# A hybrid decoder trunk on one core: the local attention's bias table is loaded ahead of the second projection's weights, and GpSimd makes its eight slopes at once

## The chip, the core and the metric

The kernel runs on one core of a Trainium2 chip. TensorE (PE) multiplies matrices, VectorE (DVE) and ScalarE (ACT) do the elementwise work, GpSimd (POOL) does a little of it, and SyncE (SP) issues nearly all transfers from HBM. Each engine works through its own list of instructions in order, and waits on semaphores for the others. The metric is the device time of one execution in microseconds (us), as the median of several. A profile of one execution gives the start and the duration of every instruction.

## The reference

The kernel computes two layers of a decoder trunk on 256 tokens of width 1024, in float32. What matters here is the beginning:

```
x = layer_norm(x, ln_in_g, ln_in_b)
memn = layer_norm(mem, ln_mem_g, ln_mem_b)
for l in range(DEPTH):
    h = x @ w_in[l]
    cq, ckv, kr, nq, kc, vc, ks, vs, kw, vw, gl = jnp.split(h, split_at, axis=-1)
    ...                         # latent attention, and sparse attention with three branches
        s = jnp.einsum('bqgrd,bkgd->bgrqk', qi, kw).astype(jnp.float32) * scale
        s = s - slopes[:, :, None, None] * dist.astype(jnp.float32)
    ...                         # output projection, cross-attention into memn, gated FFN
```

The eight heads of the sparse attention subtract a distance times a slope (one half, one quarter, ... of the distance) from their scores. The kernel holds that as a table of 8 x 256 numbers in each partition, `alibi`, made out of one table of negative distances, `neg`, which it loads as a constant.

## The kernel before

Every float32 matrix product is done as three products of numbers split into a high and a low part. A weight tile of 512 KB (`raw`, four buffers) is loaded by SP (line 122), ACT rounds it to the high part (`hi`, line 130), DVE subtracts to get the low part (`lo`, line 131), and PE multiplies. A `raw` buffer is free again when its `lo` is done, so that DVE's progress decides when SP may issue a later weight transfer.

The head of the program, in the order in which the code calls it:

1. The two token tiles `xn[0]` and `xn[1]` (128 tokens each) are loaded and normalized (`layer_norm`, lines 211 to 240). The reciprocal root of the variance is one GpSimd instruction per tile, a power of -0.5 (`rsqrt`, line 209). DVE applies it in line 240, in two halves of 512 columns. The norm of the second tile takes its sums from ACT.
2. PE transposes each half tile (`transposed`, line 247), ACT copies the result as the high part (line 250) and DVE makes the low part (line 251). Eight and six products of ones (`warm`, line 203) keep PE at work meanwhile.
3. The weights of the first projection (`w_kc`, two `raw` tiles) are loaded ahead of layer 0's list, and its products are line 487.
4. Layer 0 then runs a list of named steps written out by hand: `kc nq1 nq0 par k cmp v mem tab qk0 cq qk1 ...`. `nq1` is the second projection. `mem` normalizes the memory tokens (tile `mb`, gain `mg`), with two more GpSimd powers, and `tab` is `load_tables()`, which loads `neg`, makes `alibi` on GpSimd and loads five other tables. `qk0` is the first step that reads `alibi` (line 581).

The order of the code is not the order on the engines: a scheduler places the instructions of each engine by the times that it expects, while data dependencies and free buffers hold. So an instruction that the code calls early may stand between two that it called before.

The lines that the change and the prediction touch:

```
    def rsqrt(o, x):
        G.tensor_tensor(o, x, mhalf, op=ALU.pow)
...
            V.scalar_tensor_tensor(y[:, sl], y[:, sl], mu, g_, op0=sub, op1=ALU.mult)
            V.scalar_tensor_tensor(y[:, sl], y[:, sl], mv[:, 3:4], b_, op0=ALU.mult, op1=ALU.add)
...
        A.activation(h_, x_, AF.Copy)
        V.tensor_tensor(l_, x_, h_.bitcast(F32), op=ALU.subtract)
```

Of the kernel before, what the change touches and what calls it, by code (L numbers as in the profile page):

```python
# [10 lines left out]
F32 = mybir.dt.float32  # L11
# [3 lines left out]
ALU = mybir.AluOpType  # L15
# [3 lines left out]
P = 128  # L19
D = 1024  # L20
S = 256
# [8 lines left out]
HN = 8  # L30
# [59 lines left out]
def trunk(ctx: ExitStack, tc: tile.TileContext, a: dict, out: bass.AP):  # L90
    nc = tc.nc
    V, A, G, T = nc.vector, nc.scalar, nc.gpsimd, nc.tensor
# [4 lines left out]
    tmp = ctx.enter_context(tc.tile_pool(name="tmp", bufs=2))  # L97
# [218 lines left out]
    cok = const.tile([P, NT, HN, 16], F32, name="c_cok", tag="c_cok")  # L316
    alibi = const.tile([P, HN, S], BF16, name="alibi", tag="alibi")

    def load_tables():
        neg = tmp.tile([P, S], F32, name="neg", tag="pT", bufs=4)  # L320
        nc.sync.dma_start(neg, a["c_neg"])
        for h in range(HN):
            G.tensor_scalar(alibi[:, h, :], neg, float(8.0 * 2.0 ** (-(h + 1))), None, op0=ALU.mult)
        nc.sync.dma_start(tri, a["c_tri"])
        nc.sync.dma_start(cs, a["c_cs"])
        nc.sync.dma_start(kcs, a["c_kcs"])
        nc.sync.dma_start(ctab, a["c_ctab"])
        nc.sync.dma_start(cok, a["c_cok"])
# [67 lines left out]
    for l in range(DEPTH):  # L396
# [388 lines left out]
        def mem():  # L785
# [9 lines left out]
            "par": lambda: load_params((0,)),  # L795
            "par2": lambda: load_params((1, 2, 3)),
            "tab": load_tables,
            "cmp": lambda: e.update(vct=compress(e["c2"])),
            "mem": mem,
# [262 lines left out]
```

## Time and profile before

| what | value |
| --- | --- |
| median of three runs | 878.4 us (877.24 to 880.74) |
| the profiled execution | 879.98 us, its span 877.9 us |
| PE busy | 860.3 us, 98% of the span |
| DVE, ACT, POOL busy | 665.2, 532.5, 132.4 us |

The span runs from the first instruction to the last. A timeline row gives the start, the duration, the engine and line, what is written from what, how many instructions were merged, and in brackets how long the engine had stood idle before and what released it. A merged row's duration runs from the start of its first instruction to the end of its last. A windows row gives for a stretch each engine's busy time and the clock that TensorE was granted, 1.00 being 2.4 GHz and 0.50 being 1.2 GHz.

### The profile page before, as it was taken

How to read it: one execution, taken by the hardware profiler on the slowest of the kernel's cores; microseconds unless marked ns; L12 is line 12 of the kernel's file. 1: busy time of each engine (PE TensorE's matmuls, PEld its weight loads, DVE VectorE, ACT ScalarE, POOL GpSimd, SP SyncE). 2: the span in 40 equal slices, each digit the busy share in tenths (PEclk: the TensorE clock that was granted, in tenths of full speed). 3: DMA queues.
4: the chain of work that ended last, by engine and by line, in shares of the span. 5: the costliest groups of instructions: out<-in, count | busy, mean ns of one | idle time of the engine just before them, and what ended most of it. 6: DMA issues, size and time to landing. Idle time of an engine off the chain costs nothing.

```text
span 877.9 us, 14948 instructions
## 1 busy us (share of the span) xinstructions
PE 860.3 (98%) x5502; PEld 766.7 (87%) x5502; DVE 665.2 (76%) x1290; ACT 532.5 (61%) x1014; POOL 132.4 (15%) x140
## 2 busy tenths in 40 slices
PE   8989999999999999999999999999999999999996
PEld 5989798899989888888989998879998888888895
DVE  7789887766578877677688788968566877777777
ACT  5658764555546676666555678636573567667661
POOL 1052000000000332222300020000000033223220
PEclk9989999999999999999999999999999999999998
DMA  7944463476347756656538634446633655665641
GB/s 229 284 145 124 132 173 113 140 251 190 96 123 237 217 158 216 190 165 217 183 110 239 190 90 110 144 127 210 194 119 121 218 159 179 212 192 171 215 142 48
DMA packets 128236, 148.66 MB, mean 169 GB/s; under 512 B 6259, under 2 KB 111009, under 8 KB 128163
## 3 DMA queue, kind: packets, MB, share of 16 engines
q1 hardware_dynamic: 128159, 147.70, 54.5%
q8 instruction: 43, 0.70, 0.3%
q14 instruction: 30, 0.25, 0.1%
q10 hardware_dynamic: 4, 0.01, 0.0%
HBM read 146.64 MB, written 1.05 MB: 168 GB/s over the span
## 4 chain that ended last, share of the span: by engine, by line
PE 91%; DVE 4%; ACT 2%; DMA 2%; issue 1%; POOL 0%; SPq 0%; DVEq 0%; ACTq 0%; POOLq 0%
PE up L259 16%; PE up L261 8%; PE acc L996 5%; PE acc L997 5%; PE acc L998 5%; PE acc L170 3%; PE acc L171 3%; PE acc L169 3%; PE fill L178 2%; PE fill L179 2%; PE xq L179 2%; PE xq L178 2%; PE xq L177 2%; PE fill L171 2%; PE fill L169 2%; PE fill L170 2%
## 5 line engine op out<-in xcount | busy, mean ns | idle before, releaser
L131 DVE TENSOR_TENSOR lo<-raw,hi 128x1024 fp32r<-128x1024 f32 (+5 forms) x296 | 322.8, 1108 | 96.2 <-ACT hi L130 94.0
L130 ACT ACTIVATE hi<-raw 128x1024 fp32r<-128x1024 f32 (+5 forms) x296 | 275.8, 951 | 108.9 <-PE acc L171 34.4
L259 PE MATMUL up<-xT,hi 128*128 128x512 f32 x608 | 152.1, 392 | 0.0
L259 PEld LDWEIGHTS up<-xT,hi 128*128 128x128 f32 x608 | 110.3, 189 | 20.3
L261 PEld LDWEIGHTS up<-xT,lo 128*128 128x128 f32 x608 | 82.9, 190 | 5.9
L984 POOL TENSOR_TENSOR cv<-cv 128x256 f32<-128x256 f32 x40 | 54.2, 1356 | 218.7 <-ACT cv L982 170.0
L261 PE MATMUL up<-xT,lo 128*128 128x256 f32 x608 | 84.8, 282 | 0.0
L978 ACT ACTIVATE cv<-u,par 128x256 f32<-128x256 f32 x76 | 45.4, 598 | 49.6 <-DVE u L971 49.6
L996 PE MATMUL acc<-hi,frh 128*128 128x512 f32 x176 | 68.9, 392 | 0.0
L997 PE MATMUL acc<-lo,frh 128*128 128x512 f32 x176 | 68.8, 391 | 0.0
L998 PE MATMUL acc<-hi,frl 128*128 128x512 f32 x176 | 68.2, 389 | 0.0
L209 POOL TENSOR_TENSOR mv<-mv,mhalf 128x1 f32<-128x1 f32 x16 | 14.3, 897 | 309.0 <-DVE mv L233 158.5
L979 DVE SCALAR_TENSOR_TENSOR cv<-u,par,cv 128x255 f32<-128x255 f32 x76 | 37.6, 495 | 26.4 <-ACT cv L978 26.4
L584 ACT ACTIVATE p<-p,nm 128x128 f32<-128x128 f32 x96 | 42.6, 447 | 9.7 <-DVE nm L581 9.4
L986 ACT ACTIVATE frh<-cv 128x256 fp32r<-128x256 f32 x44 | 18.4, 418 | 37.8 <-POOL cv L984 35.4
L987 POOL TENSOR_TENSOR frl<-cv,frh 128x256 fp32r<-128x256 f32 x40 | 38.0, 952 | 20.3 <-ACT frh L986 20.3
L980 DVE SCALAR_TENSOR_TENSOR cv<-u,par,cv 128x254 f32<-128x254 f32 x76 | 37.9, 498 | 2.5
L998 PEld LDWEIGHTS acc<-hi,frl 128*128 128x128 f32 x176 | 33.0, 188 | 7.5 <-DVE frl L987 0.7
L996 PEld LDWEIGHTS acc<-hi,frh 128*128 128x128 f32 x176 | 33.1, 188 | 7.0 <-ACT frh L986 0.9
L997 PEld LDWEIGHTS acc<-lo,frh 128*128 128x128 f32 x176 | 33.1, 188 | 6.0
L177 PE MATMUL fill<-mTh,hi 128*128 128x256 f32 x128 | 37.2, 291 | 0.0
L179 PE MATMUL fill<-mTh,lo 128*128 128x256 f32 x128 | 36.6, 286 | 0.0
(279 smaller groups left out, 2151.7 us busy)
## 6 DMA issues: line engine op xcount, KB each, us to landing
raw<-in_ffn_w_up SPq DMA_DIRECT2D x88, 512.0 KB, 4.4
raw<-in_ffn_w_down SPq DMA_DIRECT2D x44, 512.0 KB, 4.3
raw<-in_xa_wkv SPq DMA_DIRECT2D x32, 512.0 KB, 3.8
raw<-in_xa_wq SPq DMA_DIRECT2D x16, 512.0 KB, 5.4
raw<-in_xa_wo SPq DMA_DIRECT2D x16, 512.0 KB, 4.2
raw<-in_w_in SPq DMA_DIRECT2D x24, 256.0 KB, 3.4
raw<-in_w_out SPq DMA_DIRECT2D x16, 256.0 KB, 4.6
raw<-in_w_out SPq DMA_DIRECT2D x8, 512.0 KB
```

The source lines that it names most:

```text
L130: A.activation(h_, x_, AF.Copy)
L131: V.tensor_tensor(l_, x_, h_.bitcast(F32), op=ALU.subtract)
L169: T.matmul(o, xh_[:, t, k], h, start=k == 0, stop=False)
L177: T.matmul(o, h[:, ms], xh_[:, :, k], start=k == 0, stop=False)
L179: T.matmul(o, lo[:, ms], xh_[:, :, k], start=False, stop=k == len(ws) - 1)
L259: T.matmul(o, h[:, ms], x2[:, k], start=k == 0, stop=False)
L261: T.matmul(o[:, 0:S], lo[:, ms], x2[:, k, 0], start=False, stop=k == len(ws) - 1)
L978: A.activation(c, u, AF.Identity, bias=pcol("cb", l, ft), scale=w_[2])
L984: E.tensor_tensor(conv[0], conv[0], conv[1], op=ALU.mult)
L996: T.matmul(o, fh[:, ts_], h[:, cs_], start=f == 0, stop=False)
L997: T.matmul(o, fh[:, ts_], lo[:, cs_], start=False, stop=False)
L998: T.matmul(o, fl[:, ts_], h[:, cs_], start=False, stop=f == NF - 1)
```

## The change

The load of `neg` and the eight multiplications that make `alibi` leave `load_tables()`. They now stand in the code just behind the first projection's weights and ahead of layer 0's list, so ahead of the weights of `nq1`.

```diff
     alibi = const.tile([P, HN, S], BF16, name="alibi", tag="alibi")
 
+    neg = tmp.tile([P, S], F32, name="neg", tag="pT", bufs=4)
+    nc.sync.dma_start(neg, a["c_neg"])
+    for h in range(HN):
+        G.tensor_scalar(alibi[:, h, :], neg, float(8.0 * 2.0 ** (-(h + 1))), None, op0=ALU.mult)
+
     def load_tables():
-        neg = tmp.tile([P, S], F32, name="neg", tag="pT", bufs=4)
-        nc.sync.dma_start(neg, a["c_neg"])
-        for h in range(HN):
-            G.tensor_scalar(alibi[:, h, :], neg, float(8.0 * 2.0 ** (-(h + 1))), None, op0=ALU.mult)
         nc.sync.dma_start(tri, a["c_tri"])
```

The same instructions are issued, in another order. On GpSimd, at the head of the program, there stood before (`mv_104` and `mv_129` are the statistics of the first and the second token tile, `mv_716` and `mv_691` those of the memory tiles):

```order
L434 MEMSET kr_190 128x64 x2
L209 ISA
L209 TENSOR_TENSOR mv_104<-mv_104,mhalf_84 128x1 [waits DVE_49]
L209 TENSOR_TENSOR mv_129<-mv_129,mhalf_84 128x1 [waits DVE_49]
L323 TENSOR_SCALAR alibi_179<-neg_744 128x256 [waits DMAHW6_49]
L323 TENSOR_SCALAR alibi_179<-neg_744 128x256 x7
L209 TENSOR_TENSOR mv_716<-mv_716,mhalf_84 128x1 [waits DVE_49]
L209 TENSOR_TENSOR mv_691<-mv_691,mhalf_84 128x1 [waits DVE_49]
```

and there stands now:

```order
L435 MEMSET kr_200 128x64 x2
L209 ISA
L209 TENSOR_TENSOR mv_104<-mv_104,mhalf_84 128x1 [waits DVE_49]
L322 TENSOR_SCALAR alibi_179<-neg_180 128x256 [waits DMAHW7_49]
L322 TENSOR_SCALAR alibi_179<-neg_180 128x256 x7
L209 TENSOR_TENSOR mv_129<-mv_129,mhalf_84 128x1 [waits DVE_49]
L209 TENSOR_TENSOR mv_726<-mv_726,mhalf_84 128x1 [waits DVE_49]
L209 TENSOR_TENSOR mv_701<-mv_701,mhalf_84 128x1 [waits DVE_49]
```

The eight multiplications moved past the power of the second token tile, which now stands behind them and behind the transfer that they wait for.

On VectorE, where the second token tile `x1_74` is finished, there stood before (`lnt_115` and `lnt_122` are the transposed halves of the first tile, `lo_170` is the low part of the first projection's second weight tile):

```order
L251 TENSOR_TENSOR xT_103<-lnt_115,xT_103 128x4x128 [waits Activation_49]
L251 TENSOR_TENSOR xT_103<-lnt_122,xT_103 128x4x128 [waits Activation_49]
L240 SCALAR_TENSOR_TENSOR x1_74<-x1_74,mv_129,fill_99 128x512 [waits DVE_49,Pool_49]
L240 SCALAR_TENSOR_TENSOR x1_74<-x1_74,mv_129,fill_100 128x512 [waits DVE_49]
L131 TENSOR_TENSOR lo_170<-raw_167,hi_169 128x1024 [waits DMAHW6_49]
```

and there stands now:

```order
L251 TENSOR_TENSOR xT_103<-lnt_115,xT_103 128x4x128 [waits Activation_49]
L240 SCALAR_TENSOR_TENSOR x1_74<-x1_74,mv_129,fill_99 128x512 [waits DVE_49,Pool_49]
L251 TENSOR_TENSOR xT_103<-lnt_122,xT_103 128x4x128 [waits Activation_49]
L240 SCALAR_TENSOR_TENSOR x1_74<-x1_74,mv_129,fill_100 128x512 [waits DVE_49]
L131 TENSOR_TENSOR lo_170<-raw_167,hi_169 128x1024 [waits DMAHW6_49]
```

One instruction of the first tile, L251 on `lnt_122`, moved between the two halves of line 240, behind the one that waits for GpSimd; `lo_170` stands behind both as before.

On SP, behind the small tables that follow the first weights, there stood before (`raw_342` is the fourth weight tile from the projections behind the first, `mg_686` the memory norm's gain):

```order
L550 DMA w2_593<-in_nsa_w2_v 128x64 [waits DMAHW5_49]
L337 DMA mg_686<-in_ln_mem_g 128x1024 [waits DMAHW6_49]
L122 DMA raw_342<-in_w_in 128x4x128 [waits DMAHW7_49,DVE_49,Activation_49]
L122 DMA raw_342<-in_w_in 128x4x128 [waits DMAHW0_49]
L122 DMA raw_414<-in_w_in 128x4x128 [waits DMAHW1_49,DVE_49,Activation_49]
```

and there stands now:

```order
L551 DMA w2_603<-in_nsa_w2_v 128x64 [waits DMAHW4_49]
L122 DMA raw_352<-in_w_in 128x4x128 [waits DMAHW7_49,DVE_49,Activation_49]
L122 DMA raw_352<-in_w_in 128x4x128 [waits DMAHW0_49]
L338 DMA mg_696<-in_ln_mem_g 128x1024 [waits DMAHW1_49]
L122 DMA raw_424<-in_w_in 128x4x128 [waits DMAHW2_49,DVE_49,Activation_49]
```

The transfer of `mg` moved behind a weight tile that waits for DVE. The transfer of `neg` stands directly behind the two tiles of `w_kc`, in seventh place of SP's list, where it stood behind the second memory tile before. PE's list is the same as before.

## Rows read from the trace of the kernel before

**Rows 1.** The page: busy time, share of the span, instructions.

```profile
PE 860.3 (98%) x5502; PEld 766.7 (87%) x5502; DVE 665.2 (76%) x1290; ACT 532.5 (61%) x1014; POOL 132.4 (15%) x140
```

**Rows 2.** PE's waits over the span: for whom, us, times, longest.

```profile
PE cmp L523 <- DVE hs L160: 4.0, 2, 3.2
```

**Rows 3.** PE's timeline, 45 to 51 us.

```profile
47.29 0.29 PE L170 MATMUL proj<-lo,xT 128*128 128x280 f32 x1
50.77 0.42 PE L523 MATMUL cmp<-c_ident,hs 34*128 34x34 f32 x2 [3.18 <-DVE hs L160]
```

**Rows 4.** VectorE's timeline, 41 to 52 us.

```profile
44.61 0.69 DVE L220 BATCH_NORM_STATS2 s<-mb 128x6 f32<-128x512 f32 x1 [2.95 <-DMA mb<-in_mem]
...
50.03 0.68 DVE L160 COPY hs<-cmp 34x512 f32<-34x512 f32 x1
50.64 1.81 DVE L131 TENSOR_TENSOR lo<-raw,hi 128x768 fp32r<-128x768 f32 x2
```

**Rows 5.** Stretches: each engine's busy us, TensorE's clock, DMA share, GB/s.

```profile
15.00:20.00 5.00, 4.58 (x32) 3.60 (x31) 5.00 (x8) 2.53 (x5) 0.00 (x0) 1.00 0.55 166
20.00:25.00 5.00, 5.00 (x45) 5.00 (x43) 4.50 (x9) 1.85 (x5) 0.00 (x0) 1.00 0.91 251
...
45.00:50.00 5.00, 2.58 (x21) 2.35 (x19) 4.90 (x7) 2.65 (x4) 4.91 (x5) 0.96 0.89 268
50.00:55.00 5.00, 4.23 (x19) 4.17 (x20) 4.97 (x14) 3.41 (x6) 4.88 (x4) 0.50 0.80 238
55.00:60.00 5.00, 5.00 (x35) 5.00 (x35) 2.78 (x9) 3.21 (x10) 1.34 (x3) 0.85 0.14 48
```

**Rows 6.** SP's timeline, 0 to 60 us: transfers issued.

```profile
16.12 0.43 SPq L337 DMA_DIRECT2D mg<-in_ln_mem_g  x1
17.89 4.52 SPq L122 DMA_DIRECT2D raw<-in_w_in  x6
...
38.07 0.65 SPq L339 DMA_DIRECT2D mb<-in_mem  x1
```

**Rows 7.** GpSimd's timeline, 0 to 60 us, and one multiplication apart.

```profile
12.15 0.56 POOL L209 TENSOR_TENSOR mv<-mv,mhalf 128x1 f32<-128x1 f32 x1 [5.47 <-DVE mv L229]
45.03 10.03 POOL L323 TENSOR_SCALAR alibi<-neg 128x256 bf16<-128x256 f32 x8 [32.32 <-DMA neg<-in_c_neg]
50.68 2.48 POOL L323 TENSOR_SCALAR alibi<-neg 128x256 bf16<-128x256 f32 x1
55.14 1.28 POOL L209 TENSOR_TENSOR mv<-mv,mhalf 128x1 f32<-128x1 f32 x2
```

**Rows 8.** VectorE's timeline, 9 to 20 us.

```profile
9.47 1.23 DVE L131 TENSOR_TENSOR lo<-raw,hi 128x1024 fp32r<-128x1024 f32 x1 [1.39 <-ACT hi L130]
...
14.69 0.69 DVE L251 TENSOR_TENSOR xT<-lnt,xT 128x512 fp32r<-128x512 f32 x1 [0.61 <-ACT xT L250]
15.30 1.40 DVE L240 SCALAR_TENSOR_TENSOR x<-x,mv,fill 128x512 f32<-128x512 f32 x2
16.62 1.22 DVE L131 TENSOR_TENSOR lo<-raw,hi 128x1024 fp32r<-128x1024 f32 x1
```

**Rows 9.** PE's timeline, 10 to 18 us.

```profile
13.03 2.76 PE L203 MATMUL lnt<-ones 128*128 128x512 f32 x6
16.14 1.33 PE L247 MATMUL lnt<-c_ident,x 128*128 128x128 f32 x8 [0.35 <-issue]
17.46 0.74 PE L487 MATMUL projt<-xT,hi 128*128 128x256 f32 x4
```

**Rows 10.** ScalarE's timeline, 0 to 60 us: first weight tiles.

```profile
10.47 1.04 ACT L130 ACTIVATE hi<-raw 128x1024 fp32r<-128x1024 f32 x1
11.72 1.15 ACT L130 ACTIVATE hi<-raw 128x512 fp32r<-128x512 f32 x2 [0.21 <-DMA raw<-in_w_in]
...
25.59 1.06 ACT L130 ACTIVATE hi<-raw 128x1024 fp32r<-128x1024 f32 x1 [1.12 <-DMA raw<-in_w_in]
```

**Rows 11.** The tile alibi: ns shortest, median, longest, first and last start.

```profile
L323 POOL TENSOR_SCALAR alibi<-neg x8: 846/1000/2482, 45.0 to 54.2; 128x256 bf16<-128x256 f32 x8
```

## The prediction

> **What bounds the kernel now.** I read the page first: PE is busy for 860.3 of 877.9 us [rows 1]. So a delay of PE's work is paid in full unless PE would have waited later anyway, and a gain can only come out of PE's waits. The view of waits, second, shows that the largest of them is 4.0 us for the tile hs, 3.2 us of it in one piece [rows 2]. PE's timeline puts that piece at 47.58 to 50.77 us [rows 3]. VectorE's timeline tells why: it stood idle for 2.95 us until the second memory tile had landed at 44.61, and hs stands in its list behind the statistics of that tile and some weight splits, so that it ran only at 50.03 [rows 4]. The windows add the other half of the price: the clock is 0.96 in the stretch 45 to 50, 0.50 in 50 to 55 and 0.85 in 55 to 60 [rows 5]. From 50.77, half the clock for about 5.7 us costs PE some 2.85 us of work. This place, wait and slow stretch, is worth about 6 us, and it hangs on a transfer: the memory tile is issued at 38.07 [rows 6] and lands 6.5 us later.
>
> The multiplications of the bias table end just then, at 55.06, and two powers of the memory norm follow at 55.14 [rows 7]. But PE's 3.2 us wait is for hs and not for them, and nothing on PE waits for the table. What the change takes away from there is worth nothing to PE, or a tenth or two where VectorE's splits run a little faster beside an idle GpSimd.
>
> **The head: GpSimd.** Before, the second token tile's power ran at 12.15 to 12.71 [rows 7], well ahead of its reader: VectorE came to line 240 of that tile at 15.30 without having waited [rows 8]. Now the power stands behind eight multiplications and their transfer. Three durations set when it runs.
>
> 1. The landing of neg. It is issued in the place of the third weight tile's first half. ScalarE takes the tile ahead of it at 10.47 without a wait, and the third tile, four times neg's 128 KB, ends a wait at 11.72 [rows 10]. So neg lands between about 10.0 and 12.1 (11.72 and some 0.4 us, my estimate for its own bytes). I take 10.5, near the lower end, as it is the first 128 KB behind the second tile.
> 2. The eight multiplications. Before they took 10.03 us together [rows 7], single ones 846 to 2482 ns with a median of 1000 [rows 11]. The long one, from 50.68 to 53.16 [rows 7], lay beside two splits on VectorE from 50.64 to 52.45 [rows 4]. At 10.5 to 14.1 VectorE runs lines 240, 239 and 251, which read one operand out of PSUM, and then it waits. So I take the short ones: 0.85 x 8 = 6.8 us; the bounds are 6.5 and 10.0.
> 3. The power itself, 0.56 us [rows 7], and 0.1 us around it.
>
> The Trainium skill says in "SBUF — State Buffer", section "Who interferes with whom", that a VectorE instruction with two operands in SBUF and a GpSimd instruction that reads SBUF exclude each other, the later one waiting until the first is done. The trace agrees: the long one ended at 53.16, 0.71 us behind the two splits. By that rule only the first split of the head, over at 10.70, could hold the table up in its new place, and the sum below would hold; were the slowing general, the eight would take 10.03 us again, which is rival A.
>
> So the power ends at 10.5 + 6.8 + 0.66 = 17.96 instead of 12.71, and line 240 of the second tile starts 2.66 us after its old 15.30. Between its halves now stands one L251 of 0.69 us [rows 8], which no longer runs early: 3.3 us later for the second half, the split lo_170 and the transposes of that half. PE starts the first projection's products at 17.46 + 3.3 = 20.8 instead of 17.46 [rows 9]. The products of ones end at 15.79 [rows 9], and from there PE has nothing to do until about 18.7. I expect its clock to fall to 0.50 there, as it did around the 3.18 us wait; at half the clock until 22 to 26 us this costs 0.9 to 2.7 us more. With the bounds of the durations the head comes 2.5 to 7.7 us later.
>
> **The stream of weights.** SP's next weight tile waits for lo_170's buffer: it was issued at 17.89, right behind the split's end at 17.84 [rows 6, 8], and goes to 21.2. All weight tiles behind it, and the memory tiles, follow it in SP's list. In addition the gain mg, 512 KB, was issued at 16.12 [rows 6], in a stretch where the transfer engines were 0.55 busy; now it stands behind that weight tile, in a stretch of 0.91 at 251 GB/s [rows 5]. In the full stream 512 KB take up to 2.0 us (512 KB over 251 GB/s), in the gaps of it nothing. I take 1.0, between the two, as the first weight tile that kept ScalarE waiting, at 25.59 [rows 10], comes soon behind it, while the stream still has some gaps. The small tables behind the memory tile gain neg's share, which nobody waits for. So the second memory tile lands 3.3 + 1.0 = 4.3 us later, hs with it, and PE resumes at 50.77 + 4.3 = 55.1.
>
> **What the second place gives back.** PE comes to it at 47.58 + 3.3 + 0.9 to 2.7 = 51.8 to 53.6, so the loss of clock at the head is hidden in this wait, and the wait is 1.5 to 3.3 us long instead of 3.2. A shorter wait should cost a shorter slow stretch. Bounds: nothing given back, or all 2.85 us. I take 1.0, nearer to nothing, since most of the wait is still there.
>
> **Sum.** 4.3 - 1.0 = 3.3 us later from 60 us on. Nothing later gives it back: PE's list is the same, its waits behind that are short, and the four powers of the memory and the table come early enough. On the profiled execution's own time this makes 879.98 + 3.3 = 883.3 us; that execution lay 1.6 us above the median of 878.4, so the forecast for the median is 881.7 us, 0.4% more. What a measurement of this kernel can tell from no change is about 0.5%, 4.4 us, so that the forecast itself is a loss too small to tell.
>
> **Rivals.**
> A, slower: GpSimd is as slow in the new place as in the old. Place: the eight multiplications at the head. Then they end at 20.5, the power at 21.2, line 240 starts 5.9 and the products 6.6 us late; with 1.5 us for mg and 1.0 given back this is 7 us, 885.4. It decides from a mean of about 1.0 us for one multiplication (8 us for all) on, where the sum passes 4.4. For it speaks the row of 10.03 us, against it that the long ones lay beside splits.
> B, no second slow stretch: PE arrives late at the wait for hs, the wait is short and the clock stays up. 4.3 - 2.85 = 1.5 us, 879.9. For it speaks that the head's slow clock shortens the wait to half; against it that even 1.5 us is a long pause for PE here.
> C, faster: the memory tile is hardly later, since the weight tiles ahead of it were held by the transfers and not by their issue; the wait for hs goes as well. PE is then late by its head alone, 3.3 + 0.9 us against a wait of 3.2 and a slow stretch of 2.85: about 1.9 us gained, 876.5. For it speaks the DMA share of 0.9 to 1.0 before 50 us, against it that SP's list stood waiting on VectorE at 17.89.
> D: A, and the second place costs as much as before or more: 10 us, 888.4.
>
> **How the numbers follow.** Forecast 0.50, with its own range of 880.0 to 883.5; A 0.18, B 0.19, C 0.07, D 0.06. Slower by over 0.5% (above 882.8): A, D and the upper fifth of the forecast, 0.34. Faster by over 0.5% (below 874.0): not even C reaches it, only C with a good draw, 0.04. Within: 0.62. The range from 878.0 to 886.5 takes in B and A and leaves out C and D and some spread of the medians.
>
> **What would show it.** In the profile of the changed kernel: eight multiplications from about 10.5 to 17.3 us, the power of the second tile behind them, VectorE waiting for GpSimd about 2.5 us ahead of line 240, PE idle from 15.8 to over 18 with a clock of 0.50 behind it, the first L487 at about 20.8, the second memory tile at about 49 and hs at about 54.3. The forecast is wrong if the multiplications take over 8 us, if neg lands after 12, if PE's wait for hs grows rather than shrinks, or if the stretch behind it keeps its clock.

## The result, and the profile after

| kernel | median of runs | range, runs | ratio to before, 95% interval |
| --- | --- | --- | --- |
| before | 878.86 us | 877.24 to 880.74, 6 | |
| changed | 884.59 us | 883.47 to 887.13, 6 | 1.0069, 1.0049 to 1.009 |
| changed, measured again (after_again) | 883.96 us | 883.72 to 886.79, 6 | 1.0055, 1.0039 to 1.0071 |

The change costs 4 to 6 us (beside after_again the kernel before took 879.72 us), where 3.3 were forecast. The time lies inside the range (878.0 to 886.5) and above the forecast of 881.7. Against the bound of 0.5% both medians fall just on the slower side, but the second interval reaches down to 0.39%. The profiled execution of the changed kernel took 887.13 us, the slowest of the six; its span is 885.0 us. That of after_again, which is the same code, took 883.83 us with a span of 881.7.

PE's busy time is almost that of before [rows 1], 1.3 us more in a span that is 7.1 us longer. So 5.8 us of the loss in this profile are PE standing still. The page of the changed kernel:

```profile
PE 861.6 (97%) x5502; PEld 768.2 (87%) x5502; DVE 665.2 (75%) x1290; ACT 532.8 (60%) x1014; POOL 130.4 (15%) x140
```

**The head.** GpSimd's timeline, 5 to 20 us (start, duration, engine and line, what is written from what, count, idle time before it and its releaser):

```profile
6.26 0.55 POOL L209 TENSOR_TENSOR mv<-mv,mhalf 128x1 f32<-128x1 f32 x1 [3.55 <-DVE mv L233]
10.02 7.06 POOL L322 TENSOR_SCALAR alibi<-neg 128x256 bf16<-128x256 f32 x8 [3.20 <-DMA neg<-in_c_neg]
17.16 0.57 POOL L209 TENSOR_TENSOR mv<-mv,mhalf 128x1 f32<-128x1 f32 x1
```

and single multiplications, shortest, median and longest in ns, where [rows 11] had 846/1000/2482:

```profile
L322 POOL TENSOR_SCALAR alibi<-neg x8: 849/850/1056, 10.0 to 16.2; 128x256 bf16<-128x256 f32 x8
```

The second tile's power ends at 17.73, not at 12.71 [rows 7]. VectorE, 13 to 21 us, which did not wait before [rows 8]:

```profile
13.51 0.69 DVE L251 TENSOR_TENSOR xT<-lnt,xT 128x512 fp32r<-128x512 f32 x1 [0.45 <-ACT xT L250]
17.76 0.75 DVE L240 SCALAR_TENSOR_TENSOR x<-x,mv,fill 128x512 f32<-128x512 f32 x1 [3.56 <-POOL mv L209]
18.43 0.69 DVE L251 TENSOR_TENSOR xT<-lnt,xT 128x512 fp32r<-128x512 f32 x1
19.03 0.74 DVE L240 SCALAR_TENSOR_TENSOR x<-x,mv,fill 128x512 f32<-128x512 f32 x1
19.68 1.22 DVE L131 TENSOR_TENSOR lo<-raw,hi 128x1024 fp32r<-128x1024 f32 x1
```

and PE, 12 to 24 us; its products began at 17.46 before [rows 9]:

```profile
12.70 2.91 PE L203 MATMUL lnt<-ones 128*128 128x512 f32 x6
18.61 0.71 PE L247 MATMUL lnt<-c_ident,x 128*128 128x128 f32 x4 [3.01 <-issue]
19.91 1.09 PE L247 MATMUL lnt<-c_ident,x 128*128 128x128 f32 x4 [0.59 <-DVE x L240]
20.65 3.54 PE L488 MATMUL projt<-xT,hi 128*128 128x256 f32 x21
```

The windows, with the columns of [rows 5] (length, then busy time of PE, PE's weight loads, DVE, ACT and POOL, the clock, the DMA share and GB/s), say two things. The clock fell to a mean of 0.90 and 0.76 in the stretches from 15 to 25, where before it was 1.00. And the transfer engines, which moved 166 GB/s from 15 to 20 before, moved 20:

```profile
15.00:20.00 5.00, 1.41 (x7) 0.54 (x6) 2.24 (x4) 2.02 (x4) 2.52 (x4) 0.90 0.09 20
20.00:25.00 5.00, 5.00 (x34) 5.00 (x35) 4.84 (x8) 0.60 (x1) 0.00 (x0) 0.76 0.60 169
45.00:50.00 5.00, 5.00 (x45) 5.00 (x44) 0.31 (x1) 2.54 (x4) 0.00 (x0) 1.00 0.86 286
50.00:55.00 5.00, 1.53 (x13) 1.30 (x11) 4.59 (x7) 2.30 (x4) 0.00 (x0) 1.00 0.76 245
55.00:60.00 5.00, 3.60 (x17) 3.54 (x18) 4.97 (x15) 3.76 (x7) 0.90 (x1) 0.66 0.74 220
60.00:65.00 5.00, 5.00 (x40) 5.00 (x39) 3.40 (x12) 3.59 (x11) 1.31 (x3) 1.00 0.25 87
```

**The stream.** SP's issues, which answer to [rows 6]. The weight tile is 3.08 us later, the gain stands behind it, and the second memory tile goes out at 41.04 instead of 38.07:

```profile
20.97 0.93 SPq L122 DMA_DIRECT2D raw<-in_w_in  x2
21.94 0.50 SPq L338 DMA_DIRECT2D mg<-in_ln_mem_g  x1
...
36.12 2.88 SPq L122 DMA_DIRECT2D raw<-in_w_in  x4
...
41.04 1.27 SPq L340 DMA_DIRECT2D mb<-in_mem  x1
```

That tile lands 9.3 us after its issue, where before it took 6.5. VectorE waits for it longer than in [rows 4] and comes to hs 5.63 us late:

```profile
50.31 0.69 DVE L220 BATCH_NORM_STATS2 s<-mb 128x6 f32<-128x512 f32 x1 [5.00 <-DMA mb<-in_mem]
...
55.66 0.68 DVE L160 COPY hs<-cmp 34x512 f32<-34x512 f32 x1
```

and PE's wait for hs has grown from the 3.18 us of [rows 3]:

```profile
51.24 0.29 PE L170 MATMUL proj<-lo,xT 128*128 128x280 f32 x1
56.40 0.53 PE L524 MATMUL cmp<-c_ident,hs 34*128 34x34 f32 x4 [4.86 <-DVE hs L160]
```

**PE along the program.** Set against before instruction by instruction, PE is 3.95 us late from 26 to 47 us, 5.63 late behind the wait for hs and 4.62 late from 60 us on, since the slow stretch behind the wait is shorter. At 500 us the same wait comes back in layer 1. It took 0.78 us before. In the changed kernel's profile it took 2.05 us, with a slow stretch behind it, and PE is 7.1 us late to the end. In after_again PE is 4.28, 4.98 and 4.05 us late at the first three places, and nothing is added in layer 1. The windows from 500 to 515 us, of the changed kernel:

```profile
500.00:515.00 15.00, 12.95 (x91) 12.59 (x90) 10.53 (x24) 9.98 (x20) 0.00 (x0) 0.89 0.52 156
```

and of after_again, with the full clock:

```profile
500.00:515.00 15.00, 14.29 (x112) 13.65 (x110) 11.90 (x41) 10.93 (x28) 0.00 (x0) 1.00 0.65 193
```

Of the twelve executions of this code eight took 883.5 to 884.7 us and four 886.0 to 887.1. The 2.5 us that come and go in layer 1 are the size of that gap. One execution of each sort was profiled, so this fits, but it is not shown for the others.

### The profile page after: what moved, and what is told of

It reads as the page before. It is cut to its first block, busy times and chain, and to the rows that moved or that the text cites. A ratio compares the mean times of both kernels' runs of the same rounds, so it can differ in the third digit from the quotient of the medians.

```text
span 885.0 us, 14946 instructions
## 1 busy us (share of the span) xinstructions
PE 861.6 (97%) x5502; PEld 768.2 (87%) x5502; DVE 665.2 (75%) x1290; ACT 532.8 (60%) x1014; POOL 130.4 (15%) x140
## 4 chain that ended last, share of the span: by engine, by line
PE 82%; DVE 7%; DMA 4%; ACT 3%; issue 1%; POOL 1%; SPq 0%; DVEq 0%; ACTq 0%; POOLq 0%
PE up L259 16%; PE up L261 8%; PE acc L997 4%; PE acc L998 4%; PE acc L999 4%; PE acc L170 3%; PE acc L169 3%; PE acc L171 3%; DVE lo L131 3%; DMA raw<-in_w_in 2%; PE xq L179 2%; PE xq L178 2%; PE xq L177 2%; PE fill L171 2%; PE fill L169 2%; PE fill L170 2%
```

## The experiments

Below, "hs" is the start of line 160 in layer 0 (50.03 before). Ratios are to the kernel before, which ran beside each of them; its median there lay between 879.72 and 880.17 us.

**1. The code again.** after_again, shown above.

> The changed kernel unaltered, for its time beside the others and a second profile. In its first profile PE lay 3.95 us behind at the wait for hs in layer 0, 4.55 us from 61 to 498 us, and 7.1 us from the like wait in layer 1 on, where hs came 1.27 us later against PE's other work and the clock fell once more. Theory A (only the head and the memory tile are the change's doing, the loss in layer 1 comes and goes): PE is 4.3 to 4.8 us behind before 498 us again, and the wait for hs in layer 1 is anything from 0.8 to 2.1 us; the median lies 4.5 to 6 us above before. Theory B (layer 1 is part of the change): again 2 us of wait and half the clock behind it, 7 us behind at the end.

Measured: 883.96 us, 4.2 us above before. Head as in the first profile (multiplications 7.05 us from 10.23), hs at 55.01. Theory A held, with both sizes a little under its bounds: PE is 3.9 to 4.1 us behind from 57 to 498 us, and the wait in layer 1 is 0.71 us.

**2. The head's queue alone.** The kernel before, with a second table's load and eight multiplications put at the change's place; the real table is made later as before.

```diff
+    neg2 = tmp.tile([P, S], F32, name="neg2", tag="pT", bufs=4)
+    nc.sync.dma_start(neg2, a["c_tri"])
+    for h in range(HN):
+        G.tensor_scalar(alibi[:, h, :], neg2, float(8.0 * 2.0 ** (-(h + 1))), None, op0=ALU.mult)
     def load_tables():
```

> The kernel before, and in addition another table of 128 KB loaded at the place of the change and eight multiplications made of it in front of the second tile's power; neg and its eight multiplications stay where they were before. Theory A: the head alone makes the loss, so it is the same 4.5 to 7 us slower than before, and the multiplications at 50 us make no difference to the changed kernel beyond 0.5 us. Theory B (freeing GpSimd at 45 to 55 us gave something back): 1 to 3 us slower than the changed kernel, so 6 to 9 us slower than before.

Measured: 884.38 us (882.9 to 887.58, 6 runs), ratio 1.0055 (1.0038 to 1.0073), hs at 55.04. GpSimd:

```profile
9.88 7.12 POOL L322 TENSOR_SCALAR alibi<-neg 128x256 bf16<-128x256 f32 x8 [3.12 <-DMA neg<-in_c_tri]
17.08 0.57 POOL L209 TENSOR_TENSOR mv<-mv,mhalf 128x1 f32<-128x1 f32 x1
50.05 10.10 POOL L328 TENSOR_SCALAR alibi<-neg 128x256 bf16<-128x256 f32 x8 [32.40 <-DMA neg<-in_c_neg]
```

The scheduler put the gain behind the weight tile here as well (issued at 21.86), so this run has the change's orders on GpSimd and on SP, and not GpSimd's alone. The early table gives the whole loss, and GpSimd's 10.1 us at the old place, still there, add nothing to it that can be seen beside after_again (theory A). The relief of that place is worth nothing that these runs can tell.

**3. Half of the multiplications early.** Four at the new place, four at the old with a load of their own.

```diff
-    for h in range(HN):
+    for h in range(4):
...
+        for h in range(4, HN):
```

> Four of the multiplications stay in front of the second tile's power, the other four go back to the old place with a load of neg of their own. Theory A (what counts is when the power is done against 15.3 us, when VectorE came to its reader before): four multiplications of 0.88 us from 10.0 end at 13.6 and the power at 14.3, nobody waits, so the head is as before and the time is that of the kernel with the table behind nq1, 0 to 2 us slower than before. Theory B (each multiplication costs its share): half of the loss, 2.5 to 3.5 us slower than before.

Measured: 881.78 us (879.62 to 883.51, 12 runs), ratio 1.0019 (1.0008 to 1.003). The four take 3.62 us, the power runs at 13.36 and the second tile's line 240 even 1.3 us earlier than before, as it now stands ahead of one L251: the head's loss is gone, since the power still comes in time. But the gain is again issued behind the weight tile, and hs runs at 51.47, 1.44 us late. The median lies 2.1 us above before, at the upper end of theory A and under that of B.

**4. The table behind the second projection's first weights.** The load and the eight multiplications as a step of their own, called behind `nq1`.

```diff
-    {'attn': 'kc nq1 nq0 par k cmp v mem tab ...
+    {'attn': 'kc nq1 alb nq0 par k cmp v mem tab ...
```

> The load of neg and the eight multiplications stand one projection later, behind the weights of nq1; in the engines' lists the second tile's power now stands ahead of the multiplications, and L251 runs early again, but mg stays behind the weight tile as in the changed kernel. Theory A (GpSimd's list holds up the second token tile, and that is the larger part): the head is as before, first L487 at 17.5, and only mg's 512 KB in the full stream is left, hs 1 to 2.4 us later than the 50.03 of before: 0 to 2 us slower than before. Theory B (the early transfer and mg's move make the loss, GpSimd's delay is hidden): 4 to 6 us slower, as the changed kernel.

Measured: 882.46 us (880.94 to 883.92, 9 runs), ratio 1.0031 (1.002 to 1.0042). The power runs at 11.93, ahead of the table, PE's head is 0.2 us early, and hs comes at 52.15, 2.12 us late, with the gain again behind the weight tile. Head and hs are those of theory A; the median, 2.7 us above before, lies between the times of A and B.

**5. The gain first.** The changed kernel, with the load of the memory gain as a step behind `par`, ahead of the weight tile that waits for VectorE.

```diff
-    {'attn': 'kc nq1 nq0 par k cmp v mem tab ...
+    {'attn': 'kc nq1 nq0 par lg k cmp v mem tab ...
...
+    def load_gain():
+        nc.sync.dma_start(mgb[0], bcast(a["ln_mem_g"], D))
```

> The changed kernel with the transfer of mg back at its old place on SP's list, ahead of the weight tile that waits for lo_170; the eight multiplications stay in front of the second tile's power. It is the other half of the kernel with the table behind nq1, where the head was free and mg late (hs 2.1 us late, 2.7 us slower). Theory A (two causes: mg late costs some 2 us at hs, the head the rest): first L487 at 20.6 as in the changed kernel, but hs at 53.0 to 53.8 instead of 55.0 to 55.7, 1.5 to 3 us slower than before. Theory B (the head is all of it, and mg was noise): hs at 55 and 4 to 6 us slower. Theory C (mg is all of it, the head is hidden in the wait for hs): hs at 50 to 51 and within 1 us of before.

Measured: 883.93 us (881.27 to 886.98, 10 runs), ratio 1.004 (1.0024 to 1.0056). The gain is issued at 14.38 and hs still runs at 55.27, as theory B said. With the head late, the gain's place is worth nothing that can be seen. The scheduler also moved three small tables of 32 KB, issued at 14.42 to 15.65 before, behind the weight tile.

**6 and 7. The memory tiles ahead of the gains,** so that VectorE's list does not wait for them, in the kernel before and in the changed one.

```diff
+        for t in (1, 0):
+            nc.sync.dma_start(mn[t], a["mem"][0, t * P:(t + 1) * P, :])
         for i, v in enumerate(("ln_mem_g", "ln_mem_b")):
             nc.sync.dma_start(mgb[i], bcast(a[v], D))
-        for t in range(NT):
-            nc.sync.dma_start(mn[t], a["mem"][0, t * P:(t + 1) * P, :])
```

> The kernel before with the four transfers of the memory norm in another order: the second memory tile first, which takes the place of mg at 16 us, then the first tile, then the gains. Theory A (hs waits for the second memory tile alone, through the statistics in VectorE's list): the wait of 3.2 us for hs falls to under 1.5 us, the clock stays at 1.00 or falls for less, and the kernel is 3 to 6 us faster than before. Theory B (a further transfer or the weight splits would hold VectorE as long): the wait stays over 2 us and the time within 1.5 us of before.

Measured: 878.82 us (877.39 to 880.18, 12 runs), ratio 0.9986 (0.9976 to 0.9997). The tile's statistics run at 33.68, 11 us early, but VectorE's list then waits at nearly the same place for a weight tile:

```profile
47.91 0.96 DVE L131 TENSOR_TENSOR lo<-raw,hi 128x768 fp32r<-128x768 f32 x1 [2.49 <-ACT hi L130]
48.91 0.68 DVE L160 COPY hs<-cmp 34x512 f32<-34x512 f32 x1
```

So it is the stream as a whole that is late, and the memory tile was only the transfer that stood last in it. PE's wait is 2.28 us, and the slow stretch behind it as long as before (theory B).

> The changed kernel with the same order of the four transfers. Theory A (the wait for hs is what hides PE's late start of 4.0 us and shrinks or grows with the memory tile): without it PE's late start is paid in full, 3.5 to 4.5 us slower than the kernel before with the memory tile first, and still not slower than the kernel before itself by more than 1.5 us. Theory B (the head has slack of its own): under 2 us between the two.

Measured: 881.89 us (879.75 to 884.98, 12 runs), ratio 1.0024 (1.0011 to 1.0038). In the profile, which is the fastest of the twelve executions, PE is 4.5 us late until hs, which runs at 52.67. Its wait there is 1.33 us, the clock stays up, and at 58 us PE is only 0.2 us later than before:

```profile
50.00:55.00 5.00, 3.67 (x30) 3.40 (x29) 3.42 (x5) 3.65 (x5) 0.00 (x0) 1.00 0.78 265
55.00:60.00 5.00, 5.00 (x41) 5.00 (x40) 5.00 (x20) 4.27 (x14) 1.98 (x2) 1.00 0.55 177
```

This is the forecast's rival B, and C's gain in the wait, as they look when they do happen: a head 4.5 us late costs nothing in that one execution. The median, 3.1 us above that of the kernel before with the same order, says that it is not so in most. That distance lies between theory A's 3.5 to 4.5 and theory B's 2.

**8. The memory step called later,** behind `tab qk0 cq`, in the kernel before.

```diff
-    {'attn': 'kc nq1 nq0 par k cmp v mem tab qk0 cq qk1 ...
+    {'attn': 'kc nq1 nq0 par k cmp v tab qk0 cq mem qk1 ...
```

> The kernel before with the step mem moved behind tab, qk0 and cq in the list. The scheduler then loads neg at 16 us, in mg's old place and behind the second tile's power, the memory tiles behind the weights of the third projection, and puts their statistics behind hs in VectorE's list. Theory A: the table early costs nothing where nobody stands behind it, and hs no longer waits for a transfer, so PE's wait for it falls under 1.5 us: 2 to 6 us faster than before. Theory B (the later memory norm holds up the cross-attention's keys instead): PE waits later for the memory tiles' transposes, and the time is within 1.5 us of before or slower.

Measured: 882.42 us (880.79 to 884.54, 12 runs), ratio 1.0029 (1.0016 to 1.0043). hs runs at 51.91, later than before, though no memory tile stands ahead of it: VectorE idles 3.15 us for a weight tile's high part, with the tables' transfers now ahead of it in the stream. Theory A failed. Between 70 and 100 us PE goes from 1.4 to 4.3 us late, at waits in the attention (0.92 and 1.24 us the longest) and in a slow stretch behind them, and not at the memory tiles' transposes that theory B named.

**9. The second power ahead of the table.** The changed kernel with one more GpSimd instruction, which reads the second tile's power and writes the first column of the slopes, so that the table must follow it. All transfers keep the changed kernel's order.

```diff
+        return mv
...
-        layer_norm(xn[t], gb, act=cfg['lnact']['in'][t])
+        mv_in = layer_norm(xn[t], gb, act=cfg['lnact']['in'][t])
...
     nc.sync.dma_start(neg, a["c_neg"])
+    G.tensor_scalar(alibi[:, :, 0], mv_in[:, 3:4].to_broadcast([P, HN]), 1.0, None, op0=ALU.mult)
     for h in range(HN):
```

> The changed kernel with one more GpSimd instruction, which reads the second tile's power and writes the first column of all eight slopes; so the table stands behind both powers, while neg's transfer stays in its new early place. Theory A (the loss enters through the second tile's power in GpSimd's list, and the rest through the gain's place in SP's list): power near 12.2, line 240 of the second tile near 15.3 or earlier, the first projection's products near 17.5 (as before), weight tile issued near 17.9, but the gain still behind it; hs 1.4 to 2.5 us later than before (51.4 to 52.5) and a median 2 to 3 us above before's, near 882. Theory B (the early table hurts wherever it stands, by GpSimd's reads beside VectorE or by neg's bytes): head 1 us or more late, and a median at 884 as the changed kernel.

Measured: 882.08 us (879.46 to 883.27, 12 runs), ratio 1.002 (1.0008 to 1.0032). GpSimd, 12 to 22 us:

```profile
12.03 0.55 POOL L209 TENSOR_TENSOR mv<-mv,mhalf 128x1 f32<-128x1 f32 x1 [5.16 <-DVE mv L229]
12.67 0.27 POOL L322 TENSOR_SCALAR alibi<-mv 128x8 bf16<-128x8 f32 x1
13.03 8.35 POOL L324 TENSOR_SCALAR alibi<-neg 128x256 bf16<-128x256 f32 x8
```

PE's head is 0.1 us earlier than before, with the table still made at the head. What is left sits in the stream: the gain goes out behind the weight tile, and VectorE shows

```profile
46.86 0.69 DVE L220 BATCH_NORM_STATS2 s<-mb 128x6 f32<-128x512 f32 x1 [4.51 <-DMA mb<-in_mem]
...
52.20 0.68 DVE L160 COPY hs<-cmp 34x512 f32<-34x512 f32 x1
```

with hs 2.17 us late and PE 1.6 us late to the end. This is theory A.

**10. Power and gain first.** Edits 5 and 9 together.

> The same, and the memory gain's transfer again ahead of the weight tile that waits for VectorE. Theory A (power and gain are the whole of the loss): hs at 49.5 to 50.6, PE's wait for it near 3, median within 1 us of before's, 879 to 881. Theory B (something else of the early table costs as well, such as neg's 128 KB ahead of the third weight tile, or the gain's place makes no difference, as it did with the power late): median 1.5 to 4 us above before's, 881.5 to 884.

Measured: 878.94 us (878.37 to 881.58, 11 runs), ratio 0.9988 (0.9976 to 1.0001). VectorE:

```profile
44.24 0.69 DVE L220 BATCH_NORM_STATS2 s<-mb 128x6 f32<-128x512 f32 x1 [2.43 <-DMA mb<-in_mem]
...
49.58 0.68 DVE L160 COPY hs<-cmp 34x512 f32<-34x512 f32 x1
```

All of the loss is gone with these two orders mended, and the table is still made early. So, within the 0.1% or so that the interval leaves, this is the whole of it: the power's place in GpSimd's list and the gain's place in SP's. As in experiment 5, the gain changed places with three small tables.

**11 and 12. The transposes of hs called later,** behind the third projection's products, in the kernel before and in the changed one.

```diff
             copy_(hs, hid[0:34, :], cfg['opt']['H'])
+            return hs
+
+        def compress_end(hs):
             pt = bank("cmp")
...
-    {'attn': 'kc nq1 nq0 par k cmp v mem tab ...
+    {'attn': 'kc nq1 nq0 par k cmp v ct mem tab ...
```

In layer 1's list the new step stands directly behind `cmp`, where the transposes were.

> The kernel before, with PE's four transposes of hs called behind the third projection's products (43 products later in PE's list) instead of ahead of them; hs itself keeps its place on VectorE. Theory A (the memory tile reaches PE only by that wait, products with their weights ready stand behind it): PE's wait for hs near 48 goes, no slow clock at 50 to 56, PE about 3 to 6 us earlier at 57, and a median of 874 to 877, unless a new wait for the weights' low parts takes over. Theory B (VectorE's list itself is late by the memory tile, and the low parts of the weights stand behind it there): PE then waits for L131 or for the low parts within 1 us of the old place, gain under 1.5 us, median 878 to 880.

Measured: 885.2 us (881.52 to 888.46, 9 runs), ratio 1.0046 (1.0027 to 1.0065). Theory A's median (874 to 877) failed. Locally it held: no wait for hs near 48, the full clock, and PE 5.8 us early at 58 us, which is what the prediction had put on that place (about 6 us). The windows of this kernel:

```profile
45.00:50.00 5.00, 5.00 (x42) 5.00 (x41) 4.84 (x7) 2.45 (x4) 4.43 (x5) 1.00 0.92 278
50.00:55.00 5.00, 5.00 (x38) 4.80 (x37) 3.85 (x5) 2.82 (x7) 4.87 (x4) 1.00 0.78 233
55.00:60.00 5.00, 4.44 (x26) 4.12 (x24) 4.10 (x16) 4.69 (x12) 1.73 (x3) 1.00 0.86 269
60.00:65.00 5.00, 3.17 (x14) 3.17 (x15) 3.64 (x12) 1.42 (x3) 1.20 (x2) 0.66 0.10 30
65.00:70.00 5.00, 5.00 (x24) 4.90 (x23) 3.25 (x6) 3.33 (x5) 0.25 (x1) 0.66 0.05 11
85.00:90.00 5.00, 1.24 (x6) 0.53 (x4) 3.70 (x20) 4.55 (x16) 0.80 (x2) 0.89 0.02 7
90.00:95.00 5.00, 3.99 (x19) 4.02 (x20) 4.32 (x22) 3.01 (x11) 0.98 (x3) 0.50 0.11 13
```

It is all given back and more from 60 to 95 us, where PE now waits for the chain that begins with those transposes. The total says nothing against the place's price; it says that the work behind hs was due.

> The changed kernel with the same move of the four transposes. Theory A (the head's 4 us and the wait for hs are two separate losses): PE loses its head of about 4 us, no wait for hs, and the median lies 3 to 5 us above transposes_later_before. Theory B (PE's list now has slack at the weights, which takes up the head's delay): median within 1.5 us of transposes_later_before.

Measured: 889.52 us (886.66 to 893.33, 6 runs), ratio 1.0106 (1.0085 to 1.0127), 4.3 us above the kernel before with the same edit. This is theory A. The head's loss stays without that wait for hs as well; the long waits behind 60 us take none of it up.

## Why the prediction was right, and where its sizes were off

The direction and the way in, GpSimd's list, were right. That the median fell inside the range owes something to luck: the range's upper part had been left for rival A, and what filled it was another loss, that of the stream and, in a part of the executions, that of layer 1.

**GpSimd's list: right, nearly to the tenth.** neg landed at 10.02 (10.5 was taken), the eight took 7.06 us (6.8), the power ended at 17.73 (17.96), line 240 started 2.46 us late (2.66), L251 stood between its halves, the products started at 20.65 (20.8) and SP issued the weight tile at 20.97 (21.2). Rival A, multiplications as slow as at the old place, is out. power_first shows its mechanism all the same: beside VectorE's splits the longest multiplication took 1.79 us instead of 0.85, and the eight 8.35. "SBUF — State Buffer" of the Trainium skill, section "Who interferes with whom", states that a VectorE instruction with two operands in SBUF and a GpSimd instruction that reads SBUF contend for a pair of ports under an exclusive lock. The trace agrees for that multiplication, which started at 16.38 and ended 0.70 us behind the split of 16.25 to 17.47; other rows show less than an exclusion (last section). With the power ahead nobody waits for the table, so it costs nothing. The upper bound of the head, 7.7 us, does not come out of its own durations, which give 8.2; nothing hangs on it.

**The head's clock: right, at the low end.** PE's products start 3.19 us late (3.39 in after_again), and behind the slow stretch PE is 3.95 us late (4.28): 0.8 to 0.9 us, at the low end of the 0.9 to 2.7. By the windows the clock was 0.50 for 3.4 us there. As forecast, the wait for hs hides this: PE stood there until hs came.

**The stream: the step that failed.** The sum takes the landing of the second memory tile, and hs, as SP's 3.3 us and 1.0 for the gain, 4.3. Measured are 5.70 us for the tile and 5.63 for hs (5.07 and 4.98 in after_again). The tile's issue was 2.97 us late, near the 3.3; but it then took 2.7 us longer to land, and the prediction had moved the landing with the issue. (In after_again the issue was 3.76 us late and the landing took 1.3 longer.) With the gain at its old place hs was still 5.24 us late (gain_first), so the 3.3 is the term that was too small. The stream lost more on its way than the first tile's delay. The kernel before issued a later run of weight tiles at

```profile
31.61 2.55 SPq L122 DMA_DIRECT2D raw<-in_w_in  x4
```

and the changed one at 36.12, 4.5 us later, where the tile at 17.89 was only 3.08 later. Before, the split that freed the buffer had waited for nothing. In the changed kernel it ended at 36.10, having waited for ScalarE, and ScalarE for another weight tile to land:

```profile
33.78 1.06 ACT L130 ACTIVATE hi<-raw 128x1024 fp32r<-128x1024 f32 x1 [0.41 <-DMA raw<-in_nsa_w_k]
34.87 1.23 DVE L131 TENSOR_TENSOR lo<-raw,hi 128x1024 fp32r<-128x1024 f32 x1 [0.21 <-ACT hi L130]
```

So here a transfer's landing held up a later transfer. After_again shows the same wait for a transfer (0.46 us). In queue_alone this rounding waited for PE instead (0.44 us), so PE's lateness may enter as well. But hs is not later where PE is later: PE is 3.95, 4.28, 4.33 and 4.72 us late ahead of the wait in the changed kernel, after_again, gain_first and queue_alone, and hs 5.63, 4.98, 5.24 and 5.01.

**The gain: right that it costs, wrong as a term to add.** The 1.0 us, taken between 0 and 2.0, was met in neither case. With the head in time and the gain late hs is 2.17 us late (power_first), a little over the upper bound; with the head late it costs nothing that can be seen (gain_first, hs at 55.27 beside 55.01 and 55.66). The two do not add: the late head alone makes hs 5.2 us late, the gain alone 2.2, both 5.0 to 5.6. The sum had 3.3 + 1.0 = 4.3.

The bytes fit the head being the dearer. In the stretch from 15 to 45 us the kernel before moved

```profile
15.00:45.00 30.00, 29.58 (x241) 28.60 (x240) 23.30 (x39) 18.04 (x30) 0.00 (x0) 1.00 0.91 259
```

and the changed one

```profile
15.00:45.00 30.00, 26.41 (x206) 25.54 (x205) 23.00 (x38) 15.70 (x27) 2.52 (x4) 0.94 0.77 207
```

so 52 GB/s less, 1.56 MB over 30 us, or 6.0 us of the stream at 259 GB/s, where hs was 5.63 us late. In the other kernels, all but one, the same window and hs go together within 1.4 us:

| kernel | GB/s, 15 to 45 us | behind, at 259 GB/s | hs later than before |
| --- | --- | --- | --- |
| after_again | 204 | 6.4 us | 4.98 us |
| gain_first | 209 | 5.8 us | 5.24 us |
| queue_alone | 207 | 6.0 us | 5.01 us |
| power_first | 238 | 2.4 us | 2.17 us |
| table_behind_nq1 | 238 | 2.4 us | 2.12 us |
| half_early | 248 | 1.3 us | 1.44 us |
| power_and_gain_first | 261 | -0.2 us | -0.45 us |
| memory_step_late | 239 | 2.3 us | 1.88 us |
| memory_first_before | 266 | -0.8 us | -1.12 us |
| memory_first_after | 214 | 5.2 us | 2.64 us |
| transposes_later_before | 254 | 0.6 us | 0.48 us |
| transposes_later_after | 204 | 6.4 us | 5.05 us |

The third column is an estimate from the second. The exception is memory_first_after, which the bytes do not explain. Of the changed kernel's 1.56 MB, 1.14 are missing from 15 to 25 us (20 and 169 GB/s instead of 166 and 251), 4.4 us of the stream by the same estimate. They were not made up before hs: the transfer engines had been 0.91 busy over the 30 us before. The remaining 0.4 MB are missing behind that; what held them is not shown. The table shows that bytes and hs go together. That the two orders are the cause was shown by mending them.

**PE's wait for hs: wrong.** It was to shrink to 1.5 to 3.3 us, and it grew to 4.86 (3.88 in after_again). This was named beforehand as what would prove the forecast wrong, and by that sign it was wrong at this place. The error is that of the stream: PE came to it at 51.54, close to the 51.8 to 53.6 that were named, and hs came 1.4 us later than the 54.3 (0.7 in after_again).

**What the second place gives back: right in size, by luck.** 1.0 us was taken, for a shorter wait. The wait was longer, and the slow stretch shorter all the same; PE went from 5.63 to 4.62 us late behind it, and from 4.98 to 4.05 in after_again. The slow stretch was 3.4 us long in both, where it had been 6.8. In gain_first and queue_alone it was 6.8, and little was given back.

**Nothing later: wrong in a part of the executions.** Layer 1's wait for hs added 2.5 us in the changed kernel's profile, in gain_first's (2.1) and in half_early's (2.2), and nothing in after_again's. In transposes_later_before, without the early table, the same place costs 2.5 us too (a wait of 1.99 us and a slow stretch), so the early table is not needed for it. No run tells what decides it.

Of the rivals, B needed a wait for hs that keeps the clock up, and only memory_first_after has one. C had the transfers hold the weight tiles, which in part they did, but it expected the memory tile to be hardly later for that; it came later than forecast. A's time (885.4) lies nearest to the first median, by another way than its own.

A version that beats before clearly was not found: memory_first_before (ratio 0.9976 to 0.9997) and power_and_gain_first (0.9976 to 1.0001) are by their ratios 0.1% faster, and the second's interval takes in no change.

## What to carry to other kernels

An instruction moved to the front of an engine's list is paid by whatever it now stands in front of: ask for every list, the queue of transfers too, which small instruction behind it somebody waits for. Where the transfer engines are nine tenths busy over a long stretch, price a delay at its front by the bytes that are not moved in it, up to the first wait that hangs on the stream: here that estimate gives 4.4 us, where hs was 5.0 to 5.6 late. Look also at what the freeing of each buffer waited for; it can be another transfer. Two causes that end in the same wait need not add, and here they did not; try each alone.

## What the runs showed of the hardware

The clock behind a wait does not follow the wait's length in these runs: behind 4.86 us (the changed kernel) it was 0.50 for 3.4 us, behind 2.28 us (memory_first_before) for 6.8 us, and behind 1.33 us (memory_first_after) it stayed at 1.00. GpSimd's multiplications and VectorE's splits did not always hold each other up in full: in memory_step_late, from 20.35 to 23.64 us, four multiplications kept their 0.85 us beside splits of 128x512 that took 0.89 instead of 0.68, where in power_first one multiplication waited out a split of 128x1024 (1.79 us). A 512 KB transfer into the full stream took 6.5 us from issue to landing in the kernel before and 9.3 us in the changed one.
